# FFN up products on x times the norm weight: the reciprocal root moved behind the products, five tall sets in each FFN

## The chip, the cores and the metric

One Trainium2 chip, one of its cores. The metric is the device time of one execution in microseconds (us), the median of several runs. Engines: PE is TensorE (matmuls), PEld its weight loads, DVE VectorE, ACT ScalarE, POOL GpSimd, SP SyncE; SP and POOL issue most of the transfers here.

## The reference

One block of a macaron network on x of 512 tokens by 1024 features, all fp32: a feed-forward network (FFN1), a mixer (short convolution and gated linear attention, left out here), a second feed-forward network (FFN2), and a last norm.

```python
D_MODEL = 1024; SEQ = 512; D_FF = 2816; EPS = 1e-6

def rmsnorm(x, g):
    y = xf * lax.rsqrt(jnp.mean(xf * xf, axis=-1, keepdims=True) + EPS)
    return (y * g)

def swiglu(x, w_gu, w_down):
    g, u = jnp.split(x @ w_gu, 2, axis=-1)
    return (jax.nn.silu(g) * u) @ w_down

x = x + 0.5 * swiglu(rmsnorm(x, norm_ffn1_g), ffn1_w_gu, ffn1_w_down)
x = x + hybrid_mixer(rmsnorm(x, norm_mix_g), ...)
x = x + 0.5 * swiglu(rmsnorm(x, norm_ffn2_g), ffn2_w_gu, ffn2_w_down)
return rmsnorm(x, final_norm_g)
```

The root of the mean is one number for each token. So it may be applied to x, or to the rows of the products x·g @ w_gu.

## The kernel before

**Numbers.** Every fp32 matrix is split into a high and a low part of a shorter type (fp32r), and a product takes three passes: high·high, high·low, low·high. For weights, SP loads a raw tile `f` (512 KB as a rule), ACT casts it to `wh` (the high part), DVE subtracts to get `wl` (the low part). For activations the two parts are called `op` here, h and l in the code.

**Layout.** x is kept feature-major, eight tiles `X` (X0 to X7) of 128 features by 512 tokens. A product is feature-major when the weights are the stationary operand, and token-major when the activations are. The down products need feature-major input (`hid`), so a token-major result is turned by transposes on PE (`turn`), into PSUM tiles named `aux`, from which ACT copies it.

**How the FFN up products are tiled.** D_FF is 22 blocks (f) of 128, each with a gate (g) and an up (u) column block. Three forms are used:
- A *group* takes two f blocks, k by k over the eight k of the input, and *singles* one column block each. These are plain products, 24 matmuls of 512 columns for one column block.
- A *set* is a Strassen-like product for two f blocks: seven products named m1, p2, q6, p5, q7, p4, p3, each of 24 matmuls of 256 columns.
- A *tall set* does the same for four f blocks. It is token-major, and each product has two halves (steps) of 12 matmuls of 512 columns, 168 matmuls in all.

The weight operands of a (tall) set are sums of raw tiles. For a11, a12, a21, a22, POOL's queue does a21 += a22, then a11 += a21, then a12 += a11, by accumulating transfers from tile to tile (`f<-f`); and DVE does a11 −= a22 (L387) for q7, in place. m1 reads a11 as loaded, q6 reads a11 after its add, p5 reads a21, p2 reads a12, q7 reads a11 after the subtraction, p3 reads a12 after its add, p4 reads a22.

**Where the norm stands.** `Norm` makes x·g in two parts; the root (`finish`, two matmuls of 512 columns with ones) is a row along the tokens. Plain products are scaled by it (`plain_pair`); for sets and tall sets DVE makes g·x·root (`normed`).

**What sets the order.** `PLAN` lists the units of weights and `STEPS` the order in which they are used; `Weights.take` has the tiles, casts and adds of a step issued two steps ahead. There are three `wh` buffers and ten `f` buffers, so a cast can't start before the step three before has ended on PE. A tall set's raw tiles are loaded some four steps ahead. Each engine runs its instructions in the order written, and SP's loads wait for a free `f` tile. FFN1 is a group of two f blocks, singles for two, four tall sets, one set; FFN2 a group, singles, a tall set, the set, three tall sets. `hid` has 22 f blocks; its last eight hold the normed x until they are overwritten.

Of the kernel before, what the change touches and what calls it, by code (L numbers as in the profile page):

```python
# [15 lines left out]
P = 128  # L16
# [87 lines left out]
PLAIN1, PLAIN2 = 4, 4  # L104
# [27 lines left out]
TALL_ORDER = ("m1", "p2", "q6", "p5", "q7", "p3", "p4")  # L132
TALL = {}


def tall(name, mat, cols, base=0):
# [6 lines left out]
    STEPS.extend((n, p) for p in TALL_ORDER for n in firsts)  # L143

# [13 lines left out]
def up_plan(up, plain, slow):  # L158

    kinds = ["tall"] * ((KF - plain) // 4)  # L160
    kinds.insert(len(kinds) if slow else 1, "set")
    f = plain
    for kind in kinds:
        if kind == "tall":
            tall((up, f), up, (f * P, DFF + f * P))
# [50 lines left out]
ffn_plan("ffn1_w_gu", "ffn1_w_down", PLAIN1, True)  # L216
mixer_plan()
ffn_plan("ffn2_w_gu", "ffn2_w_down", PLAIN2, False)
# [8 lines left out]
def block_kernel(ctx: ExitStack, tc: tile.TileContext, xT, vecs, gf, gup, wgl, wts, out):  # L227
# [79 lines left out]
    class Weights:  # L307
# [15 lines left out]
        def phase(self, early, first=6):  # L323
# [4 lines left out]
            for i in range(lo, self.end):  # L328
                n, p = STEPS[i]
                if p == "m1" and n in TALL:  # L330
                    self.loads.setdefault(i - (4, 3)[TALL[n][1]], []).append(n)
                    self.firsts.setdefault(i - (1, 0)[TALL[n][1]], []).append(n)
# [31 lines left out]
        def issue(self):  # L364
            at = self.issued
            self.fetch(at)
            for n in self.loads.get(at, ()):
                self.raw[n] = [self.dma(n + i) for i in range(4)]
# [144 lines left out]

    def rstd_rows(accs, width):
# [47 lines left out]
    class Set:  # L562
# [8 lines left out]

        def run(self, p):
            b = {"m1": "b", "p2": "a", "q6": "b", "p5": "c", "q7": "b", "p4": "b", "p3": "c"}[p]
            if self.group.joint:
                return self.run_joint(p, b)
# [6 lines left out]
            for k in range(4):  # L582
                for e in range(2):
                    s = slice(k * HW + e * P, k * HW + (e + 1) * P)
                    t = slice(k * HW, (k + 1) * HW)
                    to = o[:, e * HW : (e + 1) * HW]
                    for j, (ww, aa) in enumerate(((h, bh), (h, bl), (l, bh))):
# [9 lines left out]
        def run_joint(self, p, b):  # L597
            fresh = b not in self.bank
            two_banks = b != "b"
            if fresh:  # L600
                self.bank[b] = MM2() if two_banks else MM()
            o = self.bank[b]
            parts = self.group.get(p)
            h, l = W.take()
            for k in range(4):
                a = parts[k // 2][:, (k % 2) * S : (k % 2 + 1) * S]
                for e in range(2):
                    s = slice(k * HW + e * P, k * HW + (e + 1) * P)
                    if two_banks:
                        nc.tensor.matmul(o[:, e], h[:, s], a, start=fresh and k == 0,  # L610
                                         stop=False, skip_group_check=True)
                        nc.tensor.matmul(o[:, e, HW:], l[:, s], a[:, :HW], start=False,
                                         stop=k == 3, skip_group_check=True)
                        continue
                    to = o[:, e * HW : (e + 1) * HW]
                    for j, (ww, aa) in enumerate(((h, a[:, :HW]), (h, a[:, HW:]),
                                                  (l, a[:, :HW]))):
                        nc.tensor.matmul(to, ww[:, s], aa, start=fresh and k == 0 and e == 0 and j == 0,
                                         stop=k == 3 and j == 2, skip_group_check=True)
            if p in self.keep:  # L620
                v = T()
                nc.scalar.copy(v, o)
                self.v[p] = v
            self.done(self, p)

    class Operands:
# [5 lines left out]
        def __init__(self, b, joint=False):  # L632
            self.b = b
            self.joint = joint
            self.parts = {}
# [21 lines left out]
        def make(self, p):  # L657
            if p in self.parts:
                return
            i = self.ORDER.index(p)  # L660
            if i > 0:
                self.make(self.ORDER[i - 1])
            v = self.sum(p)
            if self.joint:
                t = [tile_of("op", [P, 1024], F32R) for _ in range(2)]
                for i in range(2):
                    a = t[i].rearrange("p (k b t) -> p k b t", b=2, t=HW)
                    vi = v[:, 2 * i : 2 * i + 2]
                    nc.scalar.copy(a[:, :, 0], vi)
                    nc.vector.tensor_tensor(out=a[:, :, 1], in0=vi,  # L670
                                            in1=a[:, :, 0].bitcast(F32), op=ALU.subtract)
                self.parts[p] = t
                return
# [61 lines left out]
    def ffn(up, down, norm, nxt, plain, at):  # L735
        xh, xl = norm.h, norm.l
        rows = []

        def finish(k):
            if k == at:  # L740
                rows.append(norm.finish())

        o = mm_group(up, KD, (0, DFF, P, DFF + P), xh, xl, extra=finish, slow=nxt is not None)
        row = rows[0]
        hid = tile_of("hid", [P, KF, S])
        xn = {}

        def normed(j, l):


            if (j, l) not in xn:
                t = slice(l * HW, (l + 1) * HW)
                f = KF - KD + 4 * j
                v = hid[:, f : f + 4, t]
                for i in range(4):
                    k = 4 * j + i
                    nc.vector.scalar_tensor_tensor(
                        out=v[:, i], in0=x[k][:, t],
                        scalar=vec[:, norm.goff + k : norm.goff + k + 1], in1=row[:, t],
                        op0=ALU.mult, op1=ALU.mult)  # L760
                xn[j, l] = v
            return xn[j, l]

        xo = Operands(normed)

        def plain_pair(f, g, u):
            s, t = T(), T()
            mul(s, g, row)
            nc.scalar.activation(s, s, AF.Silu)
            mul(t, u, row)  # L770
            mul(hid[:, f], s, t)

        xo.make("m1")
        plain_pair(0, o[0], o[1])
        xo.make("p2")
        plain_pair(1, o[2], o[3])
        for f in range(2, plain):
            g = mm_single(up, KD, f * P, xh, xl)
            u = mm_single(up, KD, DFF + f * P, xh, xl)
            if f == 2:  # L780
                xo.make("p5")
            if f == 3:
                xo.sum("q6")
# [914 lines left out]
```

## Time and profile before

| what | value |
|---|---|
| median of three runs | 1173.78 us (1173.46 to 1174.8) |
| the profiled execution | 1173.56 us, span 1171.8 us |
| PE busy | 1161.5 us, 99%, 6410 instructions |
| DVE, ACT, POOL busy | 899.6 us (77%), 643.0 us (55%), 121.6 us (10%) |
| granted PE clock | 0.999 |
| transfers | 200.07 MB, mean 171 GB/s; first slice of 40 362 GB/s |

The profile is of one execution. PE bounds the kernel: its waits for other engines are few, and FFN1 lasts to about 340 us, the mixer to 829 us, FFN2 to the end. "Idle before, releaser" in a line of a group tells how long the engine stood idle just before those instructions, and what ended it; idle time of an engine other than PE costs nothing as long as PE's operands are ready. A line such as `872.70 21.76 PE mm L704 x96` in the chain of work is a start, a length, and a count.

### The profile page before, as it was taken

How to read it: one execution, taken by the hardware profiler on the slowest of the kernel's cores; microseconds unless marked ns; L12 is line 12 of the kernel's file. 1: busy time of each engine (PE TensorE's matmuls, PEld its weight loads, DVE VectorE, ACT ScalarE, POOL GpSimd, SP SyncE). 2: the span in 40 equal slices, each digit the busy share in tenths (PEclk: the TensorE clock that was granted, in tenths of full speed). 3: DMA queues.
4: the chain of work that ended last, by engine and by line, in shares of the span. 5: the costliest groups of instructions: out<-in, count | busy, mean ns of one | idle time of the engine just before them, and what ended most of it. 6: DMA issues, size and time to landing. Idle time of an engine off the chain costs nothing.

```text
span 1171.8 us, 16449 instructions
## 1 busy us (share of the span) xinstructions
PE 1161.5 (99%) x6410; PEld 1012.3 (86%) x6410; DVE 899.6 (77%) x1081; ACT 643.0 (55%) x811; POOL 121.6 (10%) x161
## 2 busy tenths in 40 slices
PE   9999999999999999999999999999999999999997
PEld 8888888999988888789999998888888988888886
DVE  7985657879887976777797999556598566699965
ACT  6555555635452757474654577524356555575543
POOL 0101110011110110111010112000010111101100
PEclk9999999999999999999999999999999999999999
DMA  9667785647485485877566788811746777867711
GB/s 362 132 187 170 173 221 154 170 121 180 104 283 144 93 219 155 201 206 208 141 162 158 176 201 220 288 36 50 247 112 158 195 191 155 205 177 171 179 49 72
DMA packets 59006, 200.07 MB, mean 171 GB/s; under 512 B 6865, under 2 KB 6993, under 8 KB 58929
## 3 DMA queue, kind: packets, MB, share of 16 engines
q0 software_dynamic: 19424, 70.26, 31.7%
q1 hardware_dynamic: 36912, 124.27, 31.5%
q10 hardware_dynamic: 2592, 4.49, 1.0%
q8 instruction: 50, 0.82, 0.3%
q14 instruction: 28, 0.22, 0.1%
HBM read 124.55 MB, written 8.39 MB: 113 GB/s over the span
## 4 chain that ended last, share of the span: by engine, by line
PE 96%; DVE 2%; ACT 1%; issue 1%; DMA 0%; POOL 0%; DVEq 0%; ACTq 0%; POOLq 0%
PE mm L704 44%; PE mm L588 22%; PE mm L445 7%; PE mm L422 3%; PE mm L423 3%; PE mm L421 3%; PE mm L464 1%; PE mm L463 1%; PE mm L462 1%; PE aux L826 1%; PE mm L1020 1%; PE mm L1018 1%; PE mm L1019 1%; DVE wl L394 1%; PE aux L1320 1%
## 5 line engine op out<-in xcount | busy, mean ns | idle before, releaser
L393 ACT CAST wh<-f 128x1024 fp32r<-128x1024 f32 (+1 forms) x343 | 359.2, 1048 | 381.2 <-PE mm L704 120.3
L394 DVE TENSOR_TENSOR wl<-f,wh 128x1024 fp32r<-128x1024 f32 (+1 forms) x343 | 416.8, 1218 | 184.9 <-ACT wh L393 180.1
L704 PE MATMUL mm<-wh,op 128*128 128x512 f32 x1568 | 492.4, 391 | 0.0
L704 PEld LDWEIGHTS mm<-wh,op 128*128 128x128 f32 x1568 | 294.4, 188 | 60.4
L704 PE MATMUL mm<-wl,op 128*128 128x512 f32 x784 | 305.7, 390 | 0.7 <-DVE wl L394 0.7
L588 PE MATMUL mm<-op,wh 128*128 128x256 f32 x1568 | 284.6, 284 | 0.6 <-ACT tp L593 0.6
L588 PEld LDWEIGHTS mm<-op,wh 128*128 128x128 f32 x1568 | 245.0, 192 | 1.7 <-ACT tp L593 0.8
L588 PE MATMUL mm<-op,wl 128*128 128x256 f32 x784 | 222.2, 283 | 1.1 <-DVE wl L394 1.1
L362 POOL DMA_DIRECT2D f<-f x126 | 108.6, 863 | 919.4 <-DVE wl L394 336.4
L704 PEld LDWEIGHTS mm<-wl,op 128*128 128x128 f32 x784 | 147.3, 188 | 31.2 <-DVE wl L394 1.5
L588 PEld LDWEIGHTS mm<-op,wl 128*128 128x128 f32 x784 | 150.3, 192 | 1.6 <-DVE wl L394 1.5
L445 PE MATMUL mm<-op,wh 128*128 128x512 f32 x256 | 64.0, 391 | 0.0
L421 PE MATMUL mm<-op,wh 128*128 128x512 f32 x164 | 63.8, 389 | 0.0
L422 PE MATMUL mm<-op,wh 128*128 128x512 f32 x164 | 63.8, 389 | 0.0
L423 PE MATMUL mm<-op,wl 128*128 128x512 f32 x164 | 63.8, 389 | 0.0
L445 PEld LDWEIGHTS mm<-op,wh 128*128 128x128 f32 x256 | 48.0, 188 | 10.3 <-issue 0.2
L676 ACT CAST op<-hid 128x1024 fp32r<-128x1024 f32 x42 | 43.9, 1048 | 18.7 <-PE mm L704 12.7
L677 DVE TENSOR_TENSOR op<-hid,op 128x1024 fp32r<-128x1024 f32 x42 | 51.2, 1220 | 3.6 <-ACT op L676 3.4
L387 DVE TENSOR_TENSOR f<-f,f 128x1024 f32<-128x1024 f32 x28 | 34.2, 1221 | 5.6 <-DMA f<-f 4.6
L421 PEld LDWEIGHTS mm<-op,wh 128*128 128x128 f32 x164 | 30.8, 188 | 6.5
L422 PEld LDWEIGHTS mm<-op,wh 128*128 128x128 f32 x164 | 30.8, 188 | 6.4
L423 PEld LDWEIGHTS mm<-op,wl 128*128 128x128 f32 x164 | 30.8, 188 | 6.3
(283 smaller groups left out, 1146.0 us busy)
## 6 DMA issues: line engine op xcount, KB each, us to landing
f<-wts SPq DMA_DIRECT2D x219, 512.0 KB, 4.3
f<-f POOLq DMA_DIRECT2D x126, 512.0 KB, 5.0
X<-xT SPq DMA_DIRECT2D x8, 256.0 KB, 5.3
xs<-X POOLq DMA_DIRECT2D x8, 256.0 KB, 6.3
ga<-tp ACTq DMA_DIRECT2D x8, 256.0 KB, 4.9
gb<-tp ACTq DMA_DIRECT2D x8, 256.0 KB, 3.8
tp<-ga SPq DMA_DIRECT2D x8, 256.0 KB, 4.8
X<-xs POOLq DMA_DIRECT2D x8, 256.0 KB, 7.4
```

The costliest lines, as they stand in the source:

```text
L362: nc.gpsimd.dma_start(out_, a, accum_op=ALU.add)
L387: nc.vector.tensor_tensor(out=a11, in0=a11, in1=a22, op=ALU.subtract)
L393: nc.scalar.copy(h[:, :w], raw[:, :w])
L394: nc.vector.tensor_tensor(out=l[:, :w], in0=raw[:, :w], in1=h[:, :w].bitcast(F32), op=ALU.subtract)
L421: nc.tensor.matmul(o, wh, ah, start=first, stop=False)
L422: nc.tensor.matmul(o, wh, al, start=False, stop=False)
L423: nc.tensor.matmul(o, wl, ah, start=False, stop=last)
L445: nc.tensor.matmul(o[c], w[:, s : s + P], a[k], start=k == 0 and j == 0, stop=k == kt - 1 and j == 2)
L588: nc.tensor.matmul(to, ww[:, s], aa[:, t], start=fresh and k == 0 and e == 0 and j == 0, stop=k == 3 and j == 2, skip_group_check=True)
L676: nc.scalar.copy(hv, v)
L677: nc.vector.tensor_tensor(out=lv, in0=v, in1=hv.bitcast(F32), op=ALU.subtract)
L704: nc.tensor.matmul(self.bank[b][e], aa[:, c], ww, start=fresh and i == 0 and n == 0, stop=k == 3 and n == 2, skip_group_check=True)
```

## The change

1. x·g alone enters the up products. A new class `Gain` makes x·g and the sum of squares; `finish` makes the root as a column (one number for each partition, that is for each token) with four small fp32 matmuls. It is applied to token-major products, as a scalar operand of instructions that were there already (`norm.r[t]`, and `norm.minus[t]` with the sign). Since the up products of FFN1 then need x·g again for the set operands, ACT copies it to `hid` (eight copies).
2. All up products are token-major. FFN1 begins with a group of two f blocks in which the activations are stationary; five tall sets follow. FFN2 has five tall sets and one set (`Turned`: operands swapped), after the first tall set; it begins with a tall set. Singles are gone. `turn_pair` transposes the two f blocks of the group and of the set.
3. FFN2's tall sets run in `UP_ORDER`, in which p2 stands directly ahead of q7; FFN1's and the down products keep `TALL_ORDER`.
4. A tall set's raw tiles are loaded no earlier than the first step of the phase (`max(lo, ...)`), and several tall sets due at one step are loaded in turns.
5. At FFN1's end, the first two units of the down products run six of eight column blocks, then the last tall set is turned, then the other two blocks.

The diff, cut to its core:

```diff
 TALL_ORDER = ("m1", "p2", "q6", "p5", "q7", "p3", "p4")
+UP_ORDER = ("m1", "p5", "q6", "p2", "q7", "p3", "p4")
...
-def up_plan(up, plain, slow):
-    kinds = ["tall"] * ((KF - plain) // 4)
-    kinds.insert(len(kinds) if slow else 1, "set")
+def up_plan(up, first):
+    kinds = ["tall"] * ((KF - first) // 4)
+    if first == 0:
+        kinds.insert(1, "set")
...
-def ffn_plan(up, down, plain, slow):
-    units(group(up, KD, (0, DFF, P, DFF + P), slow))
-    for f in range(2, plain):
-        units(single(up, KD, f * P))
-        units(single(up, KD, DFF + f * P))
-    up_plan(up, plain, slow)
+GU = (0, P, DFF, DFF + P)
+def ffn_plan(up, down, slow):
+    if slow:
+        units(group(up, KD, GU, True))
+    up_plan(up, 2 if slow else 0)
...
-                    self.loads.setdefault(i - (4, 3)[TALL[n][1]], []).append(n)
+                    self.loads.setdefault(max(lo, i - (4, 3)[TALL[n][1]]), []).append(n)
...
+    class Gain:
+        def add(self, k, sooner=False):
...
+                for l in ls:
+                    h, w = (t[:, i * HW : (i + 1) * HW] for t in self.parts[j, l])
+                    v = x[k][:, l * HW : (l + 1) * HW]
...
+                        nc.scalar.activation(h, v, AF.Copy, scale=g)
+                    nc.vector.scalar_tensor_tensor(out=w, in0=v, scalar=g, in1=h.bitcast(F32),
+                                                   op0=ALU.mult, op1=ALU.subtract)
...
+        def finish(self):
+            for t in range(NTB):
+                nc.tensor.matmul(st[:, t : t + 1], self.acc[:, t * P : (t + 1) * P],
+                                 ones[:, 0:1], start=True, stop=True)
...
+    def ffn(up, down, hid, norm, nxt):
+        for k in range(KD):
+            nc.scalar.activation(hid[:, XN + k], x[k], AF.Copy, scale=norm.g(k))
...
+                    for t in range(NTB):
+                        a, b = (v[:, c : c + P] for v in parts[k // 4, t // 2])
+                        nc.tensor.matmul(o[t], a, wh, start=k == 0, stop=False)
+                        nc.tensor.matmul(o[t], a, wl, start=False, stop=False)
+                        nc.tensor.matmul(o[t], b, wh, start=False, stop=k == KD - 1)
...
-                        nc.scalar.activation(g[t], g[t], AF.Silu)
+                        nc.scalar.activation(g[t], g[t], AF.Silu, scale=norm.r[t])
```

**Where instructions stand, at the places that the prediction speaks of.** The first place is the head of SP's queue, the loads at the kernel's start (`X<-xT` are X0 to X7 in turn; f_117, f_125 and f_133 before, and f_117, f_126 and f_142 now, hold the group's weights for k = 0, 1 and 2 with 3; f_206 before and f_239 now those for k = 4 and 5). Before:

```order
L358 DMA f_117<-wts 128x512
L1640 DMA X<-xT 128x512 x2
L358 DMA f_125<-wts 128x512
L1640 DMA X<-xT 128x512 x2
L358 DMA f_133<-wts 128x1024
L1640 DMA X<-xT 128x512 x4
L358 DMA f_206<-wts 128x1024
```

Now:

```order
L360 DMA f_117<-wts 128x512
L1694 DMA X<-xT 128x512 x2
L360 DMA f_126<-wts 128x512
L360 DMA f_128<-wts 128x1024
L360 DMA f_130<-wts 128x1024
L360 DMA f_132<-wts 128x1024
L360 DMA f_134<-wts 128x1024
L1694 DMA X<-xT 128x512 x2
L360 DMA f_142<-wts 128x1024
L1694 DMA X<-xT 128x512 x4
L360 DMA f_239<-wts 128x1024
```

Four blocks of the first tall set (f_128 to f_134) now stand ahead of X2, X3, f_142 and X4 to X7.

The second place is ACT at the start, after the square of X1. Before (tp are squares, op the high parts of the operands):

```order
L393 CAST wh_135<-f_133 128x1024
L499 ACTIVATE op_166<-X,vec 128x512
L508 ACTIVATE tp_170<-X 128x512
L499 ACTIVATE op_166<-X,vec 128x512
L508 ACTIVATE tp_175<-X 128x512
L499 ACTIVATE op_178<-X,vec 128x512
L508 ACTIVATE tp_182<-X 128x512
L499 ACTIVATE op_178<-X,vec 128x512
L508 ACTIVATE tp_187<-X 128x512
L393 CAST wh_216<-f_206 128x1024
```

Now, from the cast of f_142 on:

```order
L400 CAST wh_144<-f_142 128x1024
L547 ACTIVATE op_183<-X,vec 128x256
L554 ACTIVATE tp_191<-X 128x512
L547 ACTIVATE op_183<-X,vec 128x256
L547 ACTIVATE op_185<-X,vec 128x256 x2
L554 ACTIVATE tp_198<-X 128x512
L547 ACTIVATE op_183<-X,vec 128x256
L547 ACTIVATE op_185<-X,vec 128x256
L554 ACTIVATE tp_205<-X 128x512
L547 ACTIVATE op_183<-X,vec 128x256
L547 ACTIVATE op_185<-X,vec 128x256
L554 ACTIVATE tp_212<-X 128x512
L765 ACTIVATE hid_119<-X,vec 128x512 x6
L400 CAST wh_251<-f_239 128x1024
```

Operands come in halves, and six copies to `hid` now stand between the last square and the cast of the group's weights for k = 4 and 5.

The third place is DVE in a tall set of FFN2. Before, with p2's low parts first (wl_8586, wl_8603), then q6's (wl_8626, wl_8642), p5's (wl_8662, wl_8678) and q7's (wl_8701):

```order
L394 TENSOR_TENSOR wl_8586<-f_8356,wh_8585 128x1024
L559 TENSOR_TENSOR hid_7836<-tp_8484,tp_8579 128x2x256
L394 TENSOR_TENSOR wl_8603<-f_8448,wh_8602 128x1024
L394 TENSOR_TENSOR wl_8626<-f_8354,wh_8625 128x1024
L387 TENSOR_TENSOR f_8354<-f_8354,f_8360 128x1024
L394 TENSOR_TENSOR wl_8642<-f_8446,wh_8641 128x1024
L798 TENSOR_TENSOR tp_8619<-mm_8623,tp_8619 128x512
L798 TENSOR_TENSOR tp_8621<-mm_8624,tp_8621 128x512
L387 TENSOR_TENSOR f_8446<-f_8446,f_8452 128x1024
L394 TENSOR_TENSOR wl_8662<-f_8358,wh_8661 128x1024
L394 TENSOR_TENSOR wl_8678<-f_8450,wh_8677 128x1024
L394 TENSOR_TENSOR wl_8701<-f_8354,wh_8700 128x1024
```

Now, with p5's (wl_8200, wl_8216), q6's (wl_8250, wl_8266), p2's (wl_8292, wl_8309) and q7's (wl_8333):

```order
L401 TENSOR_TENSOR wl_8200<-f_7968,wh_8199 128x1024
L882 SCALAR_TENSOR_TENSOR tp_8094<-tp_8094,col_7710,tp_8191 128x256 x2
L401 TENSOR_TENSOR wl_8216<-f_8060,wh_8215 128x1024
L401 TENSOR_TENSOR wl_8250<-f_7964,wh_8249 128x1024
L401 TENSOR_TENSOR wl_8266<-f_8056,wh_8265 128x1024
L401 TENSOR_TENSOR wl_8292<-f_7966,wh_8291 128x1024
L401 TENSOR_TENSOR wl_8309<-f_8058,wh_8308 128x1024
L394 TENSOR_TENSOR f_7964<-f_7964,f_7970 128x1024
L394 TENSOR_TENSOR f_8056<-f_8056,f_8062 128x1024
L401 TENSOR_TENSOR wl_8333<-f_7964,wh_8332 128x1024
```

Both subtractions (`f_7964<-f_7964,f_7970` and `f_8056<-f_8056,f_8062`) now stand directly between p2's low parts and q7's first low part, with none of the other products' low parts between. The transfers that they wait for are POOL's, the adds a12 += a11 of p2:

```order
L364 DMA f_7964<-f_7968 128x1024
L364 DMA f_8056<-f_8060 128x1024
L364 DMA f_8373<-f_8375 128x1024
L364 DMA f_7966<-f_7964 128x1024
L364 DMA f_8058<-f_8056 128x1024
```

The add f_7966<-f_7964 stands on POOL's queue after the next tall set's first add (f_8373<-f_8375).

More of the change, by code (lines that the diff above doesn't have):

```diff
@@ L366, in issue @@
             self.fetch(at)
-            for n in self.loads.get(at, ()):
-                self.raw[n] = [self.dma(n + i) for i in range(4)]
+            new = self.loads.get(at, ())
+            if len(new) > 1:
+                raw = {(n, i): self.dma(n + i) for i in (0, 2, 3, 1) for n in new}
+                self.raw.update((n, [raw[n, i] for i in range(4)]) for n in new)
+            else:
+                for n in new:
+                    self.raw[n] = [self.dma(n + i) for i in range(4)]
             for n in self.sums.get(at, ()):
@@ L595, in run, with products, __init__ @@
             self.done(self, p)
[L597 to L624, printed above, removed]
+    class Turned(Set):
+        def products(self, bh, bl, h, l):
+            return (bh, h), (bh, l), (bl, h)
     class Operands:
         ORDER = ("m1", "p2", "p5", "q6", "q7", "p3", "p4")
-        def __init__(self, b, joint=False):
+        def __init__(self, b, order_=ORDER, parts=()):
             self.b = b
-            self.joint = joint
-            self.parts = {}
+            self.order = order_
+            self.parts = dict(parts)
             self.sums = set()
@@ L659, in make @@
                 return
-            i = self.ORDER.index(p)
+            i = self.order.index(p)
             if i > 0:
-                self.make(self.ORDER[i - 1])
+                self.make(self.order[i - 1])
             v = self.sum(p)
[L664 to L673, printed above, removed]
             h, l = (tile_of("op", [P, 1024], F32R) for _ in range(2))
@@ L732, in run_sets @@
                 f()
[L735 to L783, printed above, removed]
-            plain_pair(f, g, u)
@@ L828, in turn, with turn_pair @@
                 nc.scalar.copy(hid[:, f + j], o)
+        def turn_pair(f, tiles):
+            for j in range(2):
+                o = AUX()
+                for t in range(NTB):
+                    c = (t % 2) * HW + j * P
+                    nc.tensor.transpose(o[:, t * P : (t + 1) * P], tiles[t // 2][:, c : c + P],
+                                        ident)
+                nc.scalar.copy(hid[:, f + j], o)
+        narrow = []
         def up_set(i):
-            f = [f for kind, f in UPS[up] if kind == "set"][i]
-            h = hid[:, f : f + 2]
             def done(s, p):
```

160 lines of the change are left out of this document (124 added, 36 removed).

## The prediction

> **What bounds the kernel now.** I read the busy shares first, then what TensorE (PE) waited for, then the chain of work that ended last.
>
> ```profile
> span 1171.8 us, 16449 instructions
> PE 1161.5 (99%) x6410; PEld 1012.3 (86%) x6410; DVE 899.6 (77%) x1081; ACT 643.0 (55%) x811; POOL 121.6 (10%) x161
> PE mm L588 <- DVE wl L394: 1.1, 2, 0.6
> PE aux L292 <- POOL ones L289: 1.1, 1, 1.1
> PE mm L704 <- DVE wl L394: 0.7, 1, 0.7
> PE mm L588 <- ACT tp L593: 0.6, 1, 0.6
> ```
>
> PE is busy for 99% and in the whole run waits 3.5 us for others. The kernel is a row of matmuls; two things can change its time: the number of matmuls, and new waits. The chain, all on PE there, gives the pitch (time over count) of each kind:
>
> ```profile
> 1.11 4.64 PE aux L292 x20
> 5.75 16.68 PE mm L445 x72
> 22.89 5.46 PE mm L445 x24
> 93.63 0.87 PE aux L826 x8
> 251.48 80.63 PE mm L588 x672
> 423.71 0.89 PE aux L1278 x8
> 845.01 0.23 PE aux L529
> 872.70 21.76 PE mm L704 x96
> ```
>
> A matmul of 512 columns takes 21.76/96 = 0.227 us in a tall set and 5.46/24 = 0.2275 in the group; one of 256 columns 80.63/672 = 0.120; a transpose 0.109; a record of a small fp32 matmul 0.111.
>
> **The sum, part one: PE work.** FFN1 loses four singles of 24 matmuls (96 × 0.2275 = 21.8) and a set (168 × 0.120 = 20.1) and gains a fifth tall set (168 × 0.2275 = 38.2): −3.7. FFN2 loses its group and singles, 192 × 0.2275 = 43.7, and gains a tall set, 38.2: −5.5; its set keeps its 168 matmuls of 256 columns with operands swapped. Each FFN gains 24 transposes (a fifth tall set's 16, and 8 for two blocks that now come out token-major): 48 × 0.109 = +5.2. Each finish has four fp32 matmuls, at most 8 records × 0.111 = 0.9, for two of 0.23 (L529 and L530): +0.8 for both. Together **−3.2** (−4 to −2.5).
>
> Extra ACT and DVE work (hid copies, per-token scalings in halves) costs nothing while PE has operands ready: DVE is 77% and ACT 55% busy. Where that cover fails is the rest of the sum.
>
> **Part two: FFN1's start.** The order of SP's queue now puts four blocks of 512 KB (f_128 to f_134, which the first tall set needs at about 38 us) ahead of X2, X3, f_142 and X4 to X7, which the group needs now.
>
> ```profile
> 1.24 0.90 SPq L1640 DMA_DIRECT2D X<-xT  x2
> 3.60 0.43 SPq L358 DMA_DIRECT2D f<-wts  x1
> f<-wts SPq DMA_DIRECT2D x1, 512.0 KB, 5.7
> DMA to landing us min/median/max: 3.3/5.3/6.2
> 6.00:8.00 2.00, 2.00 (x10) 1.62 (x10) 2.00 (x4) 1.85 (x4) 0.00 (x0) 1.00 0.95 333
> 8.00:10.00 2.00, 2.00 (x10) 1.66 (x9) 2.00 (x4) 2.00 (x4) 0.00 (x0) 1.00 1.03 396
> 10.00:12.00 2.00, 2.00 (x10) 1.67 (x9) 2.00 (x4) 2.00 (x4) 0.00 (x0) 1.00 1.05 417
> 10.46 0.71 ACT L499 ACTIVATE op<-X,vec 128x512 fp32r<-128x512 f32 x1
> 11.08 0.62 ACT L508 ACTIVATE tp<-X 128x512 f32<-128x512 f32 x1
> 11.60 0.71 ACT L499 ACTIVATE op<-X,vec 128x512 fp32r<-128x512 f32 x1
> 15.01 1.98 ACT L393 CAST wh<-f 128x1024 fp32r<-128x1024 f32 x2
> 870.20 1.67 DVE L757 SCALAR_TENSOR_TENSOR hid<-X,vec,row 128x256 f32<-128x256 f32 x4
> 5.06 0.48 DVE L496 TENSOR_SCALAR op<-X,vec 128x512 fp32r<-128x512 f32 x1
> L500 DVE SCALAR_TENSOR_TENSOR op<-X,vec,op 128x512 fp32r<-128x512 f32 x24 | 17.8, 746 | 1.0 <-ACT op L499 0.8
> 24.73 0.22 ACT L550 ACTIVATE st_s<-st_v 128x16 f32<-128x16 f32 x1 [0.83 <-DVE st_v L533]
> L394 DVE TENSOR_TENSOR wl<-f,wh 128x1024 fp32r<-128x1024 f32 x341 | 415.4, 1221 | 180.5 <-ACT wh L393 175.7 <-PE aux L529 4.2
> L387 DVE TENSOR_TENSOR f<-f,f 128x1024 f32<-128x1024 f32 x28 | 34.2, 1221 | 5.6 <-DMA f<-f 4.6
> ```
>
> The last two columns of the stretches are the DMA share and GB/s: from 8 us the 16 DMA engines are full at about 0.41 MB/us. Latencies of the X loads grow from 3.3 to 6.2 us in order of issue, which is a queue. The seventh transfer (3.60 + 5.7) lands at 9.3, 2.10 MB in. In the new order X2 completes 3.41 MB: 9.3 + 1.31/0.41 = 12.5; I take 12.6, then 13.3 for X3 and 14.7 for f_142, some 5 us later than before.
>
> From X2's landing ACT has two halves and a square each for X2 and X3, then the cast of f_142. A square's pitch is 0.52 (11.08 to 11.60), an operand's 0.62; a half of one I estimate at 0.40, between 0.22 (16 columns) and 0.62. That is 2.6 us; the cast ends at 16.3 to 16.6, its low part on DVE (1.22) at 17.7. PE can use two matmuls before it, so in effect k = 2 begins at 17.2. Its step k = 1 ends at 5.75 + 24 × 0.2275 + 0.45 = 11.6, where 0.45 is the start's own delay: X0's operand is made in halves on DVE, four operations of 256 columns (1.67 for such four, L757) for two (0.48 and 0.74 before, 1.22). Stall 5.6.
>
> The second stall is ACT's order. Behind that cast stand eight halves, four squares (5.3 us), then six hid copies of the rest (6 × 0.61 = 3.7), and only then wh_251 (0.94), which is k = 4, 5. It ends at 26.2 to 26.5; DVE has L688 there and then wl_252, about 27.7. PE, which has k = 2, 3 and the finish behind it at 23.7, runs four matmuls on wh alone, so waits 27.7 − 0.9 − 23.7 = 3.1. Start together 0.45 + 5.6 + 3.1 = **+9.2**. With X2, X3 and f_142 landing as before, ACT's order alone gives 0.45 + 1.1 = 1.6, as the hid copies would end before PE gets there: the low end. High end 11, if the squares and copies pitch a tenth slower.
>
> The idle 5.6 us could cost more than itself. The 20 small matmuls at 1.11 take 0.232 each, those at 423.71 take 0.111: PE starts at half its pace, for 4.6 us or less (the granted clock reads 1.00 in every stretch, so that column doesn't show it). Half pace after the first stall would add some 2 us to k = 2, 3, which the second stall takes up, since ACT sets its end: nothing in the sum. By the Trainium skill ("TensorE: Matmul & The Clock Gate", Part 1) an idle window of about 3.4 us halves PE's clock, and 3.4 us of activity restores it. By that the sum would also stay; without the second stall it would be about 1.7 us higher.
>
> **FFN1's end.** Two down products go to aux banks while the last tall set is turned between them; they wait for ACT copies of 0.6: +0.3 (0 to 1).
>
> **Part three: FFN2's tall sets.** With UP_ORDER p2 stands directly ahead of q7. q7's weights are a11 −= a22 (L387, now L394), which must not start until the DMA a12 += a11 has read a11, and that add may not start until p2's low part is made.
>
> ```profile
> 874.12 1.22 DVE L394 TENSOR_TENSOR wl<-f,wh 128x1024 fp32r<-128x1024 f32 x1
> 875.64 0.85 POOL L362 DMA_DIRECT2D f<-f  x1 [4.20 <-DVE wl L394]
> 878.51 0.85 POOL L362 DMA_DIRECT2D f<-f  x1 [2.02 <-DVE wl L394]
> f<-f POOLq DMA_DIRECT2D x1, 512.0 KB, 4.5
> 886.64 1.22 DVE L387 TENSOR_TENSOR f<-f,f 128x1024 f32<-128x1024 f32 x1
> f<-f POOLq DMA_DIRECT2D x126, 512.0 KB, 5.0
> 895.20 0.86 POOL L362 DMA_DIRECT2D f<-f  x1 [15.83 <-ACT tp L802]
> f<-f POOLq DMA_DIRECT2D x1, 512.0 KB, 6.3
> ```
>
> Before, the add of 875.64 landed at 880.1 and the subtraction came at 886.64: 6.5 us to spare, with q6 and p5 between. Now, counting from the end of q6's first step, which frees the third wh buffer for p2's second: cast and low part 2.4, issue 0.3, landing 4.5, subtraction 1.2, and wl_8333 behind it on DVE 1.2, together 9.6 to 9.7. q7's first step starts three steps later, 3 × 12 × 0.2275 = 8.2, and has one matmul (0.23) before it needs wl_8333: stall 1.25 us for each of four tall sets. In the first, ACT also has operand copies, a table load and the root ahead of the casts: 2.1. Together **+7.1**. The 4.5 is the row I take, since no weight block comes free there for SP to load. With loads beside, as at 895.20, it is 6.3, which makes 7.1 + 5 × 1.8 = 16; the low end is 0, if casts start earlier.
>
> FFN2's begin costs nothing that I can find: SP's order has the first tall set's blocks ahead during the mixer, and its operands are made from x there.
>
> **Sum:** 1173.56 (span plus 1.8 around it) − 3.2 + 9.2 + 0.3 + 7.1 = **1187 us**; the median of the runs shown is 0.2 above that execution. What a measurement can tell from no change is 0.2%, 2.3 us.
>
> **The rivals.**
> - The start is paid, q7's chain isn't: 1173.56 − 3.2 + 9.2 + 0.3 = 1180. For it: DVE already waits for adds at L387 (5.6 us idle, 4.6 for DMA) while PE doesn't; against it, that slack was 6.5 us and is now negative.
> - Only q7's chain is paid, the start costs 1.6: 1179.4. It needs X2 to pass the blocks issued ahead of it.
> - The adds land in 6.3 us: 1187 + 5 × 1.8 = 1196. For it the row at 895.20, where SP loads ran beside; against it the two adds at 875.64 and 878.51, which overlap and take 4.5 each. The Trainium skill ("DMA: Bandwidth & Descriptors", Queues, rings and completion order) has each DMA engine take turns between the queues with work, which would put an add beside SP loads at a part of the rate; the 6.3 beside the 4.5 agrees.
> - Not slower: landing is each transfer's own latency, at both places. X2 then lands 3.3 us after issue (start 1.6), adds in 3.4 as single loads do elsewhere (q7: 0.9 in the first set, else 0): 1173.2, and without them PE work alone, 1170.4. It decides once X2 lands before about 8 us. Against it: the X latencies that grow with every issue.
>
> **How the numbers follow.** Forecast 0.50 (1184 to 1190), start only 0.17, q7 only 0.10, slow adds 0.09, not slower 0.14, of which 0.08 is faster by over 0.2% and 0.06 within it. The range 1177 to 1194 takes in the first three and a part of the fourth; outside it stay 0.14 below and 0.05 above. Slower 0.86.
>
> **What would show it.** In the profile after: PE waits near 11.6 for an operand or wh of X2 or f_142 (about 5.6 us), again near 24 for wh_251 or wl_252 (3.1); X2's landing at 12.6; PE waits at the tall matmul line for DVE once in each FFN2 tall set (1.2 to 2.1), with the subtraction's wait ended by a DMA of f<-f; PE's busy time some 3 us lower. It would be wrong if X2 lands by 8, if SP loads meet the adds, or if the added ACT work delays casts elsewhere in FFN2, which I took as hidden.

## The result, and the profile after

The changed kernel takes 1204.61 us (median of four runs, 1203.24 to 1207.6), the kernel before 1173.71: a ratio of 1.0265 (95% interval 1.0244 to 1.0286). Forecast were 1187 us and the range 1177 to 1194. The direction was right; the loss is 31 us and not 13.

The page of the changed kernel begins so:

```profile
span 1202.2 us, 16380 instructions
PE 1171.2 (97%) x6350; PEld 1011.8 (84%) x6350; DVE 888.6 (74%) x1050; ACT 668.9 (56%) x855; POOL 133.1 (11%) x170
```

PE's waits in it (engine, line, who is waited for: us in total, times, longest us):

```profile
PE mm L731 <- DVE wl L401: 11.2, 7, 2.3
PE mm L786 <- ACT wh L400: 4.9, 2, 4.2
PE mm L731 <- ACT wh L400: 3.1, 3, 1.7
PE mm L786 <- DVE op L544: 1.1, 1, 1.1
PE mm L787 <- DVE wl L401: 0.7, 1, 0.7
```

PE has 60 instructions fewer than before and yet is busy for 9.7 us longer; and it waits 20 us at two places, the group of FFN1 (L786, L787: 6.7) and the tall sets of FFN2 (L731: 13.7; the other 0.65 us of the first row is one wait in the mixer, where the kernel before waits 0.67). The busy time is the first hint that matmuls ran slower somewhere. Two marks in the chains of both kernels split the loss: the mixer's stretch of 144 tall matmuls began at 391.07 and begins now at 401.82 (+10.75: FFN1), the down products of FFN2 at 1064.35 and now at 1094.65 (+30.3, so +19.55 from the mixer's mark on).

**FFN1's start.** The chain of work at the start (start us, length, what):

```profile
4.56 7.90 DMA X<-xT
12.48 0.91 ACT op L547 x2
15.23 0.94 ACT wh L400
16.21 1.22 PE mm L786 x2
18.70 0.43 PE mm L787
22.13 0.23 PE mm L787
26.70 1.23 DVE wl L401
28.88 0.43 PE mm L787
```

And stretches of 2 us: the busy time of PE, PEld, DVE, ACT, POOL and, in the last three columns, the granted PE clock, the DMA share and GB/s:

```profile
10.00:12.00 2.00, 2.00 (x9) 1.31 (x7) 0.00 (x0) 0.00 (x0) 0.00 (x0) 1.00 1.04 409
18.00:20.00 2.00, 2.00 (x6) 1.54 (x5) 2.00 (x5) 2.00 (x5) 0.00 (x0) 0.50 1.06 272
28.00:30.00 2.00, 2.00 (x6) 1.58 (x7) 2.00 (x2) 1.99 (x3) 0.86 (x1) 0.59 0.48 90
```

X2 was issued at 4.56 and landed 7.90 later, at 12.46; the forecast said 12.6. From 8 to 12 us ACT and DVE have next to nothing to do. Then the clock: after the wait until 16.21 a matmul of 512 columns takes 0.43 us and not 0.23, and the granted clock reads 0.50. It comes back at about 21.5, and goes again after two short waits near 26 and 27.

**FFN2's tall sets.** The chain through one q7:

```profile
967.20 1.06 ACT wh L400
968.28 1.24 DVE wl L401
969.81 5.05 DMA f<-f
975.00 1.08 issue
976.08 1.23 DVE wl L401
977.35 5.51 PE mm L731 x23
```

Two stretches of 4 us by engines, columns as above, the first beside that chain and the second behind another q7's wait:

```profile
970.00:974.00 4.00, 4.00 (x19) 3.33 (x18) 1.23 (x1) 1.10 (x2) 0.67 (x1) 1.00 1.02 192
1066.00:1070.00 4.00, 3.50 (x9) 2.81 (x10) 4.00 (x6) 2.63 (x4) 0.00 (x0) 0.57 0.57 141
```

The three adds ahead of one more q7, in POOL's timeline:

```profile
920.74 0.86 POOL L364 DMA_DIRECT2D f<-f  x1 [9.43 <-issue]
923.03 0.86 POOL L364 DMA_DIRECT2D f<-f  x1 [1.44 <-DVE wl L401]
925.26 0.86 POOL L364 DMA_DIRECT2D f<-f  x1 [1.36 <-DVE wl L401]
```

And their issues, with the median us from issue to landing:

```profile
f<-f POOLq DMA_DIRECT2D x3, 512.0 KB, 6.3
```

This is the chain of the forecast link by link: p2's cast and low part, the add, the subtraction (DVE's 1.08 at 975.00, shown as issue), q7's low part, PE. But the add, the second of p2's two, takes 5.05 us here and up to 6.6 in the other tall sets, and not 4.5. While adds run the DMA engines are full (share 1.02) at some 200 GB/s, half of what loads reach: one add of 0.52 MB holds them all for about 2.6 us (0.52 over 0.2), and these are issued 2.2 us apart. And behind three of the five q7 waits PE runs at half clock again.

### The profile page after: what moved, and what is told of

It reads as the page before. It is cut to its first block, busy times and chain, and to the rows that moved or that the text cites. A ratio compares the mean times of both kernels' runs of the same rounds, so it can differ in the third digit from the quotient of the medians.

```text
span 1202.2 us, 16380 instructions
## 1 busy us (share of the span) xinstructions
PE 1171.2 (97%) x6350; PEld 1011.8 (84%) x6350; DVE 888.6 (74%) x1050; ACT 668.9 (56%) x855; POOL 133.1 (11%) x170
## 4 chain that ended last, share of the span: by engine, by line
PE 84%; DMA 6%; DVE 4%; issue 3%; ACT 2%; SPq 0%; DVEq 0%; POOLq 0%; ACTq 0%; POOL 0%
PE mm L731 43%; PE mm L649 20%; DMA f<-f 5%; PE mm L452 4%; DVE wl L401 2%; PE aux L840 1%; PE mm L430 1%; PE mm L428 1%; PE mm L429 1%; PE mm L470 1%; PE mm L471 1%; PE mm L469 1%; ACT wh L400 1%; DMA tp<-ga 1%; PE mm L1072 1%
## 5 line engine op out<-in xcount | busy, mean ns | idle before, releaser
L731 PE MATMUL mm<-wh,op 128*128 128x512 f32 x1792 | 567.8, 394 | 3.1 <-ACT wh L400 3.1
L731 PEld LDWEIGHTS mm<-wh,op 128*128 128x128 f32 x1792 | 338.6, 189 | 74.4 <-ACT wh L400 4.8
L731 PE MATMUL mm<-wl,op 128*128 128x512 f32 x896 | 351.7, 393 | 11.2 <-DVE wl L401 11.2
L649 PE MATMUL mm<-op,wh 128*128 128x256 f32 x1344 | 243.6, 284 | 0.2 <-ACT tp L654 0.2
L649 PEld LDWEIGHTS mm<-op,wh 128*128 128x128 f32 x1344 | 209.8, 192 | 1.0 <-ACT tp L654 0.4
L731 PEld LDWEIGHTS mm<-wl,op 128*128 128x128 f32 x896 | 169.6, 189 | 48.3 <-DVE wl L401 14.1
L649 PE MATMUL mm<-op,wl 128*128 128x256 f32 x672 | 190.5, 284 | 1.1 <-DVE wl L401 1.1
L649 PEld LDWEIGHTS mm<-op,wl 128*128 128x128 f32 x672 | 128.7, 192 | 1.6 <-DVE wl L401 1.5
L428 PE MATMUL mm<-op,wh 128*128 128x512 f32 x100 | 39.1, 391 | 0.0
L430 PE MATMUL mm<-op,wl 128*128 128x512 f32 x100 | 38.9, 389 | 0.0
L429 PE MATMUL mm<-op,wh 128*128 128x512 f32 x100 | 38.9, 389 | 0.0
L452 PE MATMUL mm<-op,wh 128*128 128x512 f32 x128 | 31.9, 391 | 0.0
L452 PEld LDWEIGHTS mm<-op,wh 128*128 128x128 f32 x128 | 23.9, 188 | 5.0
L470 PE MATMUL mm<-wl,op 128*128 128x512 f32 x64 | 25.0, 391 | 0.3 <-DVE wl L401 0.3
L469 PE MATMUL mm<-wh,op 128*128 128x512 f32 x64 | 25.1, 392 | 0.0
L842 ACT COPY hid<-aux 128x512 f32<-128x512 f32 x40 | 21.5, 593 | 6.4 <-PE aux L840 6.4
```

Of the source, the lines that this page charges most:

```text
L428: nc.tensor.matmul(o, wh, ah, start=first, stop=False)
L429: nc.tensor.matmul(o, wh, al, start=False, stop=False)
L430: nc.tensor.matmul(o, wl, ah, start=False, stop=last)
L452: nc.tensor.matmul(o[c], w[:, s : s + P], a[k], start=k == 0 and j == 0, stop=k == kt - 1 and j == 2)
L649: nc.tensor.matmul(to, ww[:, s], aa[:, t], start=fresh and k == 0 and e == 0 and j == 0, stop=k == 3 and j == 2, skip_group_check=True)
L731: nc.tensor.matmul(self.bank[b][e], aa[:, c], ww, start=fresh and i == 0 and n == 0, stop=k == 3 and n == 2, skip_group_check=True)
```

## The experiments

All are edits of the changed kernel. The marks are in us: the long stretch of 168 matmuls in FFN1's first tall set, the mixer's stretch of 144, and FFN2's down products, each by the start of its first instruction on PE. (The chain counts a step from where the one before it ended, so its starts lie 0.1 to 0.3 later.) Each ratio is to runs of the kernel before that were taken beside the edit; their medians lie between 1173.7 and 1175.2.

| kernel | median | ratio to before (95%) | first tall | mixer | down |
|---|---|---|---|---|---|
| before | 1173.71 | 1 | | 390.9 | 1064.1 |
| changed | 1204.61 | 1.0265 (1.0244 to 1.0286) | 46.0 | 401.7 | 1094.4 |
| e1 loads behind X | 1205.93 | 1.0271 (1.0248 to 1.0293) | 41.8 | 401.8 | 1095.7 |
| e2 p2 before q6 | 1191.24 | 1.0146 (1.0131 to 1.0161) | 44.9 | 400.6 | 1081.4 |
| e3 q7 in a21's tile | 1191.88 | 1.0147 (1.0130 to 1.0164) | 45.3 | 401.0 | 1081.9 |
| e4 waits filled | 1198.47 | 1.0202 (1.0187 to 1.0217) | 45.2 | 400.9 | 1087.8 |
| e5 four sets p5 between | 1189.63 | 1.0134 (1.0116 to 1.0151) | 46.0 | 401.7 | 1083.3 |
| e6 five sets p5 between | 1184.35 | 1.0083 (1.0068 to 1.0098) | 45.0 | 400.6 | 1075.2 |
| e7 loads, hid copies | 1198.54 | 1.0202 (1.0176 to 1.0228) | 36.4 | 396.3 | 1090.6 |
| e8 e7 and pool order | 1206.28 | 1.0275 (1.0258 to 1.0292) | 36.4 | 392.1 | 1097.3 |
| e9 all repairs | 1174.79 | 1.0002 (0.9993 to 1.0011) | 36.2 | 391.9 | 1068.4 |
| e10 quarter adds | 1185.44 | 1.0097 (1.0083 to 1.0110) | 45.3 | 401.0 | 1076.1 |
| e11 hid copies late | 1206.25 | 1.0266 (1.0247 to 1.0286) | 45.5 | 401.2 | 1098.4 |

**e1: the loads behind X.**

```diff
-self.loads.setdefault(max(lo, i - (4, 3)[TALL[n][1]]), []).append(n)
+self.loads.setdefault(max(lo + 3 * (lo == 0), i - (4, 3)[TALL[n][1]]), []).append(n)
```

> The changed kernel, with the first tall set's eight blocks of FFN1 loaded behind X0 to X7 and the group's weights, as the loads stood before. Theory (the blocks ahead of X2 hold up the start: 4.6 us of waiting at k = 2, about 2 us at k = 4, and two stretches at half PE clock of about 2 us each): the start's loss falls from some 11 to under 3 us, so about 1195 us. Rival (ACT's order sets the start, the loads only fill time that ACT loses anyway): k = 4 still begins near 27 us, about 1202.

Neither came out. The wait at k = 2 goes and the first tall set comes 4.2 us sooner: half of what the theory had, since the wait at k = 4 grows, and more than the rival had, since k = 4 begins at 21.8 and not near 27. And nothing is left of it at the mixer, so the kernel is no faster. Its waits show both:

```profile
PE mm L786 <- ACT wh L400: 2.6, 1, 2.6
PE aux L1218 <- DVE g L1203: 2.8, 1, 2.8
```

Its chain, where the mixer begins:

```profile
355.60 8.20 DMA tp<-wgl
```

And ACT's timeline at the start:

```profile
16.43 4.39 ACT L765 ACTIVATE hid<-X,vec 128x512 f32<-128x512 f32 x7
20.72 2.93 ACT L400 CAST wh<-f 128x1024 fp32r<-128x1024 f32 x3
```

ACT makes seven hid copies (4.39 us) before the cast that PE waits for. And the mixer's gate weights (`wgl`) land at 363.80, 8.20 us after their issue, behind a row of weight blocks; PE waits 2.8 us for what is made from them. In the kernel before they were loaded near 312, as SP's timeline there shows:

```profile
312.50 0.33 SPq L1140 DMA_DIRECT2D tp<-wgl  x1
```

The change also opens the mixer's pool `tp` last and no longer second, a line of the full diff that the prediction passed over.

**e11: the hid copies behind the group's casts, alone; e7: with e1's edit.**

```diff
-        for k in range(KD):
-            nc.scalar.activation(hid[:, XN + k], x[k], AF.Copy, scale=norm.g(k))
+        def copies():
+            for k in range(KD):
+                nc.scalar.activation(hid[:, XN + k], x[k], AF.Copy, scale=norm.g(k))
...
+            copies()
             norm.finish()
```

> The changed kernel, only with the hid copies behind the casts of the group's weights; the loads stay ahead of X2. Theory: the wait at k = 2 and the half clock behind it stay (6 us), the waits at k = 4 (1.5 us) and their half clock (1.7 us) go: the first tall set begins near 42.7 us for 46, and the time is about 1201.5. Rival (the wait at k = 2 takes all that time whatever ACT does next): 1204.

> The changed kernel with the first tall set's loads behind X0 to X7 and the copies of x times g to hid behind the casts of the group's weights. Theory (ACT's order makes the wait at k = 4): the first tall set begins at about 37 us for 46 in the changed kernel and 41.8 with the loads alone; but what is gained beyond 3 us is lost again near 362 us, where the mixer's gate weights land at 364 us whatever FFN1 does: 1203 to 1206. Rival (that wait moves with FFN1): about 1197.

Copies late alone move the first tall set by 0.5 us only; with the loads behind X it is 9.6 us, more than the two apart (4.2 and 0.5). Each edit by itself leaves the other queue to hold the group up. In e11 k = 4 no longer waits, but a wait of 0.9 us stands behind the group instead, where the group's own scaled tiles are turned:

```profile
PE mm L790 <- ACT wh L400: 4.9, 1, 4.9
PE aux L855 <- DVE tp L799: 0.9, 1, 0.9
```

e7's time, 1198.54, lies between the two theories: 5.4 of the 9.6 us reach the mixer's mark. The wait for `wgl` came with FFN1 (at 357 and not at 362), 2.5 us long, with half clock behind it.

**e8: e7 with the mixer's pools in the order of before.**

```diff
-    with phase("small2", f=10, v=4, qk=2, g=1, y=1, small=1, tp=6):
+    with phase("small2", f=10, tp=6, v=4, qk=2, g=1, y=1, small=1):
```

> As the kernel before it in this call, with the mixer's pool of small tiles (tp) opened second again and not last, so that the mixer's gate weights are loaded near 312 us, as before the change. Theory: the wait near 362 us goes, and the start's gain of some 9 us is kept: about 1195 us. Rival (the wait there has another cause, such as DVE's backlog): 1202 to 1206.

Right at the mixer, wrong in the sum: the mixer's mark is at 392.1, so the whole 9.6 us arrive, and FFN2 gives back more. PE's longest wait there:

```profile
PE mm L731 <- ACT op L703: 9.9, 1, 9.9
```

ACT's timeline:

```profile
833.84 5.00 ACT L766 ACTIVATE hid<-X,vec 128x512 f32<-128x512 f32 x8 [1.36 <-DVE acc L555]
838.75 1.03 ACT L703 CAST op<-hid 128x1024 fp32r<-128x1024 f32 x1
```

FFN2's eight hid copies start at 833.84 only, after the sum of squares, all in one piece, and PE waits 9.9 us for the operand made from them. I read this so: with `tp` second, the tiles of the mixer's last squares lie where FFN2's `hid` will be, and FFN2 now begins with a tall set, which needs `hid` while these tiles are in use. That would explain the changed pool order; the row shows whom the copies waited for (DVE's last `acc`, L555), not where the tiles lie.

**e2: q6 between p2 and q7; e3: the difference for q7 in another tile.**

```diff
-UP_ORDER = ("m1", "p5", "q6", "p2", "q7", "p3", "p4")
+UP_ORDER = ("m1", "p5", "p2", "q6", "q7", "p3", "p4")
```

> The changed kernel, with FFN2's tall sets in the order m1, p5, p2, q6, q7, p3, p4, so that q6's two steps (5.5 us) lie between p2 and q7. Theory (q7 waits for the adds a12 += a11 in flight: 15.9 us of PE waits in five tall sets, and three stretches at half clock, 5.3 us): both go, about 1184 us. Rival (the waits come from DVE and ACT being loaded with per-token scalings): they move to another product, and the time stays above 1198.

```diff
-                    s3 = a11
+                    s3 = a21 if TALL[n][0][0] == "ffn2_w_gu" else a11
                     if p == "q7":
-                        nc.vector.tensor_tensor(out=a11, in0=a11, in1=a22, op=ALU.subtract)
+                        nc.vector.tensor_tensor(out=s3, in0=a11, in1=a22, op=ALU.subtract)
```

> The changed kernel with its order of products kept, but in FFN2 the difference a11 - a22 for q7 is written into a21's tile (no longer needed after p5), so that the subtraction has no add in flight to wait for. Theory (the wait is for the add that still reads a11): the q7 waits go although p2 stays directly ahead of q7, about 1184 us. Rival (casts for q7 start too late with p2 there, whatever the add does): the waits stay, above 1198.

Both take about 13 us off, where 20 were expected. e3 keeps p2 directly ahead of q7 and takes away only the add that the subtraction waited for: the waits in the later tall sets vanish, so they were waits for that add. What e2 has left in the tall sets, by its waits:

```profile
PE mm L731 <- ACT tp L818: 4.6, 2, 2.6
```

And e3, its longest wait and, from the chain ahead of that cast, an add:

```profile
PE mm L649 <- ACT wh L400: 3.2, 1, 3.2
877.72 8.18 DMA f<-f
```

In e2, q6 stands directly ahead of q7 and both use one PSUM bank, so q7 waits until ACT has copied q6's result out (L818), in the first two tall sets. In e3, the first weights that FFN2 itself loads are issued at 862 us and not at 847, an add for the set falls together with the next one (879.44) and a load (877.9) and takes 8.18 us, and the set waits 3.2 us for its cast. That the loads come later because a21's tile is held longer is read from the code, not tested. Both edits also keep a wait in the first tall set and some half clock, so neither reaches 1184.

**e5 and e6: p5 between q6 and q7, in four tall sets or all five.**

```diff
-            tall((up, f), up, (f * P, DFF + f * P), order_=UP_ORDER if first == 0 else TALL_ORDER)
+            tall((up, f), up, (f * P, DFF + f * P), order_=TALL_ORDER)
...
-            at_step(((up, UPS[up][0][1]), 1, "p5"), norm.finish)
+            at_step(((up, UPS[up][0][1]), 1, "m1"), norm.finish)
```

(e6; e5 keeps UP_ORDER where f is 0, and the finish after p5.)

> The changed kernel; in FFN2 only the first tall set keeps the order with p2 directly ahead of q7, the other four run m1, p2, q6, p5, q7, p3, p4, where p5 stands between q6 and q7 and q6 and p5 between p2 and q7. Theory (q7 needs two products between it and p2 for the add in flight, and one between it and q6, since both use one PSUM bank and q6's result must be copied out first): the four lose all their q7 waits (11.5 us) and the half clock behind them (3.7 us), about 1189 us. Rival (half the time of the waits is due to ACT's and DVE's added scalings): above 1194.

> The changed kernel with the order m1, p2, q6, p5, q7, p3, p4 in all five tall sets of FFN2, and the root's four small matmuls after m1. Theory: the first tall set loses its q7 wait too (4.4 us and 1.6 us of half clock), and pays some 2 us to have p2's operands, which come from the last four features of the mixer, earlier: about 1185 us. Rival (that order costs the first tall set as much as it saves, the mixer's last features being late): 1189 to 1192.

Both came out as the theory had them, 1189.6 for 1189 and 1184.35 for 1185. In e6, of its tall sets' waits FFN2 has only these left, in the first tall set:

```profile
PE mm L731 <- DVE op L704: 0.8, 1, 0.8
PE mm L731 <- ACT op L703: 0.2, 1, 0.2
```

**e10: p2's adds of a quarter of the size** (the rest of a12's sum is left out).

```diff
-                self.add(a12, a11)
+                self.add(a12[:, :256], a11[:, :256])
```

> The changed kernel, in which FFN2's adds a12 += a11 move only the first 256 of 1024 columns (128 KB for 512), so a part of the weights' sums is left out; the order of everything stays. Theory (the length of the add's transfer, 2.6 us on all DMA engines and up to three adds in a row, sets q7's wait): each add lands some 2 us earlier for itself and as much for one ahead of it, so of 15.9 us of waits in FFN2 some 12 go, and the half clock with them: about 1188 us. Rival (the chain of casts and low parts sets it, the landing is a fixed 4.5 us whatever the size): above 1198.

Its add issues in FFN2's tall sets, with size and median us to landing:

```profile
f<-f POOLq DMA_DIRECT2D x10, 128.0 KB, 2.7
```

And PE's waits for low parts (L733 is the tall sets' matmul line here):

```profile
PE mm L733 <- DVE wl L401: 1.9, 4, 0.8
```

The ten small adds land in 2.7 us, and with every instruction in its place the kernel takes 1185.44 us, 19 less. One of the four waits of that row, 0.6 us, is the mixer's; so of FFN2's 10.6 us of waits for low parts 1.2 are left, and of its 3.1 us of waits for casts none. So the length of the adds makes q7's wait; casts and low parts alone nearly fit.

**e4: PE kept busy in its waits.**

```diff
+    def keep_warm(n):
+        o = AUX()
+        for _ in range(n):
+            nc.tensor.matmul(o[:, :P], ones, ones, start=True, stop=True)
...
+                    if k in (2, 4):
+                        keep_warm(16 if k == 2 else 8)
...
+            if p == "q7" and s == 0 and isinstance(self.warm, int):
+                keep_warm(self.warm)
```

(`self.warm` is 10 in FFN2's tall sets.)

> The changed kernel, with small matmuls on ones added where PE waits: 24 (about 5.3 us) at FFN1's start and 10 (2.2 us) ahead of q7 in each of FFN2's tall sets. No wait is removed; PE is kept busy in it. Theory (after a wait of some 2 us or more PE runs at half clock for about 3.4 us, which costs some 4 us at the start and 5 us in FFN2): the half clock goes and what it cost with it, less what later waits take up, about 1197 us. Rival (the half clock is a reading that costs nothing, or later waits take all of it up): 1204 to 1207.

The edit takes no cause of a wait away, it adds matmuls of no use, and the kernel gets 6 us faster (1198.47). From the mixer's mark to the down products it takes 686.9 us for 692.8 in the changed kernel, 5.9 less. Of FFN2's three stretches at half clock two are gone; the third stays, at 866.4, behind a wait of 2.0 us. That is some 3.2 us (an estimate, from the matmuls' pitch in such a stretch: 1.6 for each). The rest is that waits and added matmuls together take less time than the waits did; why, no run shows. So the half clock has a price, but not all of the 6 us is that price. FFN1's start gains 0.7 only. Two of its stretches, of 4 us:

```profile
16.00:20.00 4.00, 4.00 (x22) 3.13 (x22) 3.83 (x8) 4.00 (x10) 0.00 (x0) 1.00 1.05 284
28.00:32.00 4.00, 4.00 (x15) 3.19 (x15) 3.86 (x8) 2.65 (x4) 1.73 (x2) 0.73 0.78 185
```

The clock is 1.00 where it was 0.50, k = 2 and 3 are done sooner, and PE then waits longer at k = 4 (2.0 us), with half clock behind that. At the start, then, a later wait does take up what the clock had cost.

**e9: all repairs.** e1, e7 and e6 together, and the gate weights in two tiles of pool `v`, which are free before the mixer begins:

```diff
-        gl_raw = T()[:, : KD * RANK].rearrange("p (k r) -> p k r", r=RANK)
+        gl_raw = tile_of("v", [P, S])[:, : KD * RANK].rearrange("p (k r) -> p k r", r=RANK)
...
-        gup_f = T()
+        gup_f = tile_of("v", [P, S])
```

(and `vt`, which takes the other tiles of `v`, is made after them)

> The changed kernel with all repairs: the first tall set's loads behind X0 to X7, the hid copies behind the casts of the group's weights, FFN2's tall sets in the order m1, p2, q6, p5, q7, p3, p4, and the mixer's gate weights in two tiles of the pool v, loaded before the mixer's weights. Theory (all of the loss was waits and half clock; the change itself saves 3.2 us of PE work): 1204.6 less 9.6 at the start and 20.3 in FFN2 is 1174.7, within 1172 to 1177, that is no change against the kernel before, since some 2 us of waits at both starts remain. Rival (the added ACT and DVE work costs time on its own): above 1180.

The page's row of engines:

```profile
PE 1161.6 (99%) x6350; PEld 1007.2 (86%) x6350; DVE 888.4 (76%) x1050; ACT 669.1 (57%) x855; POOL 129.9 (11%) x170
```

And three of PE's waits:

```profile
PE mm L790 <- DVE op L544: 1.4, 1, 1.4
PE mm L469 <- ACT wh L400: 1.0, 1, 1.0
PE mm L470 <- DVE wl L401: 0.8, 1, 0.8
```

1174.79 us, the sum of the parts (that it fits to 0.1 is luck, with runs from 1173.4 to 1177.9), and a ratio of 1.0002 (0.9993 to 1.0011): no difference from the kernel before. All 31 us were waits and what the clock lost behind them; ACT's 26 us and POOL's 8 us more work than before cost nothing by themselves. The 3.2 us less of PE work don't show in PE's busy time, 1161.6 us as before. The profiled execution is the slowest of the eleven, 1177.9 us, and has one stretch at half clock (741.4 to 744.8) behind two of the waits above. Taken matmul by matmul, from start to start, it has some 3.5 us less of work than the kernel before, 5.6 more of waits and 1.7 of half clock. So the work was saved, and in that execution new waits took it. No version here beats the kernel before.

## Why the prediction was wrong

The step that failed is in part three: the adds of q7's chain were given the landing of one that has the engines nearly to itself, and the half clock behind waits was given no term in FFN2.

- **PE work, −3.2.** Right: some −3.5 in the trace of the changed kernel, counted as in e9 (an estimate; the whole sum stands below).
- **The queue at FFN1's start.** Right: landing in order of issue, X2 at 12.46 (12.6 forecast), X3 and f_142 within 0.3 of 13.3 and 14.7. The total was a little low, and close by luck: +9.2 forecast, and the two edits of e7 give back 9.6 while some 1.7 us of waits stay. The parts were not as forecast. The start's own delay is 1.1 for 0.45, the first stall 4.2 for 5.6, the second 1.3 for 3.1, all by the waits' rows, and two stretches at half clock, 4.4 us together (an estimate from the matmuls' pitch in them), had no term.
- **"Half pace after the first stall ... nothing in the sum."** For that stall this held (e4). The step failed behind it: the short waits at 26 and 27 us brought a second stretch, and the same thought was never put to FFN2's stalls, which were forecast at 1.25 us each. There it costs 4.8 us in three stretches (the same estimate).
- **"The 4.5 is the row I take."** This is the mis-sized term: 7.1 us forecast, 13.7 us of waits measured. The row at 875.64 was of adds 2.87 us apart. In the new order p2's two come 2.2 us apart (1.2 in the first tall set, at 857.98 and 859.18, and 1.5 in the fifth), in the second tall set behind a third add, and each holds all DMA engines for 2.6. So the second lands 5.05 to 6.6 us after its issue, with no SP load running beside it. In the first, third and fifth tall set, 4.5 plus what of 2.6 is left when the second is issued gives the landing to 0.2 us (6.1, 5.1 and 5.8). In the other two it comes 1.1 and 1.4 us later than that. There, and only there, a load of instructions (queue q8) falls among the adds, 16 KB that take 1.35 and 1.55 us, and the last packets of the adds end about 1 us behind the rest; that the one makes the other is not tested. The rival of slow adds had about the size (6.3, 1196 us) for another reason. The transfers in flight were in the order listing, with the next tall set's add ahead of p2's two; their service time was in the profile before, as a full share and GB/s:

```profile
880.00:882.00 2.00, 2.00 (x10) 1.67 (x9) 1.62 (x2) 1.71 (x2) 0.00 (x0) 1.00 1.08 207
```

- **FFN1's end, +0.3.** About right: in the changed trace two matmuls near 248 us start 0.26 and 0.11 us late.
- **The rivals.** That q7's chain is hidden fell with e3 and e10. That X2 passes the blocks ahead fell with the landing at 12.46. "Not slower" fell with both.
- **What was missing:** the pool line of the diff. It costs nothing in the changed kernel, where FFN1 is late anyway, and 4.2 us as soon as FFN1 is repaired (e7: a wait of 2.5 and the half clock behind it).

The sum as measured, again matmul by matmul from start to start: PE work −3.5, waits +23.5 (7.4 of them at FFN1's start and 15.6 in FFN2; a wait is some 0.2 us longer so than in the rows, which count from a matmul's end), half clock 4.4 and 4.8, and 1.0 spread over many small steps. That is the 30.3 us between the profiled executions. The split is an estimate, as each kind's usual pitch stands for its work.

## What to carry to other kernels

An operation in place that follows a transfer reading the same tile is a wait, and its price takes in the service time of the transfers in flight ahead of it, not only the latency of one that ran alone. Before moving a product, ask three things: which add must land, which bank must be emptied (e2), which tile comes free later (e3). And where two queues each delay one consumer, repair both before judging either: e1 and e11 alone gained nothing in the end, together they gave 9.6 us to FFN1.

## What the runs showed of the hardware

- PE's granted clock falls to 0.50 behind waits much shorter than I had thought worth a term. In the changed kernel it fell behind waits of 4.2 us, of 0.7 and 0.7 close together, of 1.7 and 2.3, of 0.4 and 2.0, and of 2.2; it did not behind 1.0 and 2.0 or a single 1.8. A stretch lasts 3.4 us in its trace, the first 6.8, and costs 1.5 to 2.8. The Trainium skill ("TensorE: Matmul & The Clock Gate", Part 1) says half rate after an idle window of about 3.4 us that runs free of the kernel; the 3.4 us agree, and the waits here show that less idle time than a whole window is enough at times.
- The length of a wait alone doesn't decide it. In e1 FFN2 has the changed kernel's instructions, and its q7 waits are the same within half a microsecond, yet there the clock fell behind 1.3 and 2.0 and behind the single 1.8, and did not behind the last 2.2. The same stretch of 4 us, just behind the second tall set's q7 wait, in the changed kernel and in e1:

```profile
936.00:940.00 4.00, 4.00 (x21) 3.26 (x20) 3.40 (x5) 1.69 (x3) 0.00 (x0) 1.00 0.78 259
936.00:940.00 4.00, 4.00 (x13) 3.23 (x12) 2.12 (x3) 1.77 (x2) 0.00 (x0) 0.65 0.87 273
```

- So a few microseconds can differ between executions of one kernel. The changed kernel's runs spread over 4.4 us, the kernel before's beside them over 1.3. That waits near the edge make this spread is argued, not shown.
- Accumulating transfers from tile to tile run at about 200 GB/s with all 16 DMA engines full (192 at a share of 1.02), loads at 410 (409 at 1.04).
